# Input projection with its column groups in another order, a gelu in two parts, and low weight parts made by an adding DMA

## The chip, the core and the metric

The kernel runs on one core of one Trainium2 chip. The metric is the device time of one execution in microseconds (us). Three executions of the kernel before took 1475.19, 1468.30 and 1471.88 us; the median is 1471.88 us.

## The reference

The model is a decoder step of two layers for a prompt of 512 tokens and 8 sequences of 4 new tokens. Each layer has a mixing part and a feed-forward part (FFN). In the mixing part one input projection of 1024 to 2048 columns feeds four mixers of width 256, whose outputs are concatenated and go through an output projection:

```python
h = rms_norm(x, p['g_mix_pre'])
z = h @ p['w_in']                                   # 1024 -> 2048
a, ga, u, vb, q, k, v, xd = jnp.split(z, IN_SPLITS, axis=-1)   # eight groups of 256 columns
ya, conv_new = conformer_conv(a, ga, conv_prev, ...)           # depthwise convolution of width 31, LayerNorm
yb, v_rows = chunk_sgu(gelu(u), gelu(vb), ...)                 # u * (tril(W) LN(v) + b)
o = attend(q, k, v, lam)                                       # differential attention
yd, pool_new = pool_mix(xd, ...)                               # window means
mix = jnp.concatenate([ya, yb, yc, yd], axis=-1) @ p['w_out']  # 1024 -> 1024
x = x + rms_norm(mix, p['g_mix_post'])
...                                                            # then the SwiGLU FFN
```

All of it is float32.

## The kernel before

A float32 product is made of three products of a rounded type (fp32r): each operand is split into a high part (the rounded value) and a low part (the rest), and high by high, high by low and low by high are added in PSUM. For a weight tile, `split` (line 189) makes the high part `whi` by a cast on ScalarE (ACT, line 194) and the low part `wlo` by a subtraction, on VectorE (DVE) unless another engine is named (line 197). `whi` and `wlo` are rings of four buffers each in the pool `wp`, and a tile of 128 columns of w_in takes one buffer of each. A group of 256 columns is two tiles. Its raw weights (1 MB, a ring of two buffers) are loaded by the queue of SyncE (SP).

The function `mixing` (line 354) writes the input projection as 15 steps, one for each tile of 128 columns and one for the group at 1536 (the attention's v, which takes two tiles in one step). `order` (line 406) fixes the groups: columns 0 and 256 (convolution), 1280 (k), 1024 (q), 1536 (v), 1792 (pooling), 512 (gating's u), 768 (gating's v). The loop at line 719 does the first 256 tokens of step u, and then the other 256 prompt tokens with the 32 sample tokens (288 columns) of step u-2. So a tile is in use for two steps after its own, and its buffer goes to the tile four places later. The mixers are generators (`conv`, `attention`, `gating`, `pooling`): `advance` moves each active one on between the steps, and those in the list `urgent` are written under a higher priority. A scheduler that simulates the program then fixes the final order of each engine's instructions, from these priorities and from what is ready. PSUM has two banks `acc` for the projections, three `ps`, two `s` and one `oT`, mostly for the attention.

`gating` is started when the last group, 768, is done. It applies gelu to u and v together (lines 592 to 594), then LayerNorm and a product over chunks, then the multiplication by u (line 615), and writes `yb`. The convolution's taps run on DVE (line 427); the rest of `conv` (lines 440 to 464) turns the result, normalises it and writes `ya`. `attention` writes `yc` and `pooling` writes `yd`.

`project_last` (line 1273) then does the output projection: eight turns of 24 matmuls of 512 columns, over the k-tiles in the order `W_OUT_ORDER` = 6, 7 (`yd`), 0, 1 (`ya`), 2, 3 (`yb`), 4, 5 (`yc`). The first turns go to different token tiles, so two of them can be open at once in the `acc` banks.

Of the kernel before, what the change touches and what calls it, by code (L numbers as in the profile page):

```python
# [9 lines left out]
F32R = mybir.dt.float32r  # L10
BF16 = mybir.dt.bfloat16
I32 = mybir.dt.int32
AF = mybir.ActivationFunctionType
ALU = mybir.AluOpType
# [27 lines left out]
AP = 3  # L42

W_OUT_TURNS = [(0, 0), (1, 0), (0, 1), (1, 1), (2, 0), (2, 1), (3, 0), (3, 1)]
W_OUT_ORDER = (6, 7, 0, 1, 2, 3, 4, 5)

PACE_T = 1.0
PACE_A = 0.8
# [74 lines left out]
def trunk(ctx, tc, A, O):  # L123
    nc = tc.nc
    V, S, G, T, SY = nc.vector, nc.scalar, nc.gpsimd, nc.tensor, nc.sync
# [16 lines left out]
    def ps():  # L142
        return psx("ps")
# [210 lines left out]
    def mixing(l, mp, early):  # L354
# [35 lines left out]
        def ev_qk(nm, c, f):  # L390
# [18 lines left out]
            (1280, [(10, ev_qk("k", 0, 10)), (11, ev_qk("k", 1, 11))]),  # L409
            (1024, [(8, ev_qk("q", 0, 8)), (9, ev_qk("q", 1, 9))]),  # L410
            (1536, "v"),
            (1792, [(14, ev_copy(dext[0], 14, 1.0, 15)), (15, ev_copy(dext[1], 15, 1.0, 15))]),
            (512, [(4, ev_copy(uv[:, 0], 4)), (5, ev_copy(uv[:, 1], 5))]),
            (768, [(6, ev_copy(uv[:, 2], 6)), (7, ev_copy(uv[:, 3], 7))]),
        ]


# [12 lines left out]
                    yield  # L430

        convs = []

        def conv():
            for c in range(2):
                while len(convs) <= c:
                    yield
                yield from convs[c]
            o = ps()
            for c in range(2):  # L440
                T.transpose(o[:30, 128 * c:128 * c + 128], hext[c][:, SEQ:SEQ + 30], ident)
            cn = mp.tile([128, SEQ], F32, tag="pt", bufs=3, name="cn")[:, :256]
            S.copy(cn[:30], o[:30, :256])
            SY.dma_start(O[4][l, 0], cn[:30])
            yield
            xn = mp.tile([128, 4, 256], F32, tag="xn", bufs=1, name="xn")
            for t in range(4):
                o = ps()
                for c in range(2):
                    T.transpose(o[:, 128 * c:128 * c + 128], out[c][:, 128 * t:128 * t + 128], ident)  # L450
                mean, r = ln_stats(mp, o[:, :256], 128, "m")
                V.tensor_scalar(xn[:, t, :], o[:, :256], mean, r, op0=ALU.subtract, op1=ALU.mult)
                yield
            y = yp.tile([128, 2, 2, SEQ], F32R, tag="y", name="ya")
            for c in range(2):
                o = ps()
                for t in range(4):
                    T.transpose(o[:, 128 * t:128 * t + 128], xn[:, t, 128 * c:128 * c + 128], ident)
                zh, th = out[c], hext[c][:, 0:SEQ]
                S.activation(zh, o, AF.Identity, scale=pf[:, 72 + c:73 + c], bias=pf[:, 74 + c:75 + c])  # L460
                S.activation(th, zh, AF.Tanh)
                V.scalar_tensor_tensor(zh, th, 1.0, zh, op0=ALU.add, op1=ALU.mult)
                hilo(y, c, zh)
                yield
            Y[0] = y
# [102 lines left out]
        def gating():  # L568
# [20 lines left out]
                mm(o[64 * (h % 2):64 * (h % 2) + 64, 128 * (h // 2):128 * (h // 2) + 128], gr[:, 64 * h:64 * h + 64], wt[:, h, :])  # L589
            V.tensor_tensor(bsg, o[:, :256].rearrange("p (c t) -> p c t", c=2), bsg, op=ALU.add)  # L590
            yield
            for f in (2, 0):
                S.activation(uv[:, f:f + 2], uv[:, f:f + 2], AF.Gelu)
            S.activation(zs[:, 4:8, :], zs[:, 4:8, :], AF.Gelu)
            yield
            vn = mp.tile([128, 4, 256], F32, tag="xn", bufs=1, name="vn")
            for t in range(4):
# [7 lines left out]
            for c in range(2):  # L605
                o = acc()
                for n in range(4):
                    for hh in range(2):
                        h = 2 * c + hh
                        mm(o[64 * hh:64 * hh + 64, 128 * n:128 * n + 128], vn[:, n, 64 * h:64 * h + 64], wt[:, h, :])  # L610
                t = uv[:, 2 + c, :].rearrange("p (n t) -> p n t", n=4)
                V.scalar_tensor_tensor(t, o.rearrange("p (n t) -> p n t", n=4), pf[:, 77 + c:78 + c],
                                       bsg[:, c:c + 1, :].to_broadcast([128, 4, 128]), op0=ALU.mult, op1=ALU.add)
                tf = uv[:, 2 + c, :]
                V.tensor_tensor(tf, tf, uv[:, c, :], op=ALU.mult)
                hilo(y, c, tf)
                yield
# [73 lines left out]
        def load(c0):  # L691
            if c0 == 1536:
                r = rp.tile([128, 8, 256], F32, tag="raw", name="raw")
                SY.dma_start(r, w[:, c0:c0 + 256].rearrange("(k p) f -> p k f", p=128))
                pairs[c0] = [split(r[:, 4 * i:4 * i + 4, :], [128, 4, 256], V) for i in range(2)]
            else:
                pairs[c0] = raw_cols(w, c0, V, early.get(c0), None, G if c0 == 0 and early else None)

        def do_v(t, P, dst):
            o = acc()  # L700
# [18 lines left out]
        for u in range(n + LAG):  # L719
# [19 lines left out]
            if b >= 0:  # L739
# [9 lines left out]
                if c0 == 256 and i == 0:  # L749
                    convs.append(taps(0))  # L750
                    active.append(conv())
                if c0 == 256 and i == 1:
                    convs.append(taps(1))
                if c0 == 1024:
# [5 lines left out]
                        active.append(keys_out())  # L760
                if i == "v":
                    done.add("v")
                if c0 == 768 and i == 1:
                    active.append(gating())
                    urgent.append(active[-1])
# [709 lines left out]
```

## Time and profile before

The profiled execution took 1470.1 us, of which 1468.2 us lie between its first and its last instruction (the span).

| | |
|---|---|
| span | 1468.2 us |
| profiled execution | 1470.1 us |
| median of three | 1471.88 us |
| TensorE (PE) busy | 1393.0 us, 95% |
| DVE busy | 816.3 us, 56% |
| ACT busy | 490.4 us, 33% |
| GpSimd (POOL) busy | 253.9 us, 17% |
| mean granted TensorE clock | 0.981 |

The busy time of PE is that of pipelined matmuls whose ends are modelled, so a stretch in which PE is always busy can still be slow: the granted clock (1.00 is 2.4 GHz, 0.50 is 1.2 GHz) and the spacing of matmuls of one size tell that. What counts for the change is not the share over the whole span but the stretches of the mixing part: the input projection, the stretch between its last matmul and the steady output projection, and the output projection itself. In layer 0 these are about 32 to 156 us, 156 to 181 us and 181 to 232 us; in layer 1 about 758 to 883 us, 883 to 908 us and from there on.

### The profile page before, as it was taken

What the parts mean: (1) busy time and instruction counts of PE and PEld (TensorE: products, weight loads), DVE (VectorE), ACT (ScalarE), POOL (GpSimd) and SP (SyncE); (2) the same over time, 40 slices, a digit from 0 to 9 for tenths busy, and PEclk for the clock granted to TensorE, in tenths of its full rate; (3) what the DMA queues carried; (4) which work ended last, traced back from release to release, by engine and by line L of the source; (5) the groups of instructions that cost most, each with busy time, mean ns of one, the idle gap of its engine ahead of it and who ended that gap; (6) DMA issues with size and microseconds to landing.
All of it is one profiled execution on the core that took longest, in us unless ns stands there. A gap on an engine that the chain in (4) does not pass through costs nothing.

```text
span 1468.2 us, 22964 instructions
## 1 busy us (share of the span) xinstructions
PE 1393.0 (95%) x9274; PEld 1085.7 (74%) x9274; DVE 816.3 (56%) x1624; ACT 490.4 (33%) x972; POOL 253.9 (17%) x271
## 2 busy tenths in 40 slices
PE   6999798989999999999989997989899999999997
PEld 6988677856676777777779886787566677777775
DVE  4997577866424323433669856867564333333344
ACT  4345444322224221222333464433222332222231
POOL 1000245443300000000210004434342000000003
PEclk9999998999999999999999999999999999999999
DMA  6220336786859731323432213378767596213132
GB/s 206 93 87 30 131 117 213 257 299 230 286 177 292 238 137 58 104 69 128 152 115 73 73 53 109 128 244 299 274 235 266 182 299 210 100 58 115 58 133 90
DMA packets 155204, 235.60 MB, mean 160 GB/s; under 512 B 8880, under 2 KB 116410, under 8 KB 155098
## 3 DMA queue, kind: packets, MB, share of 16 engines
q1 hardware_dynamic: 136522, 166.76, 34.8%
q0 software_dynamic: 18432, 67.12, 12.8%
q8 instruction: 73, 1.20, 0.3%
q14 instruction: 33, 0.27, 0.1%
q10 hardware_dynamic: 144, 0.26, 0.0%
HBM read 222.07 MB, written 12.04 MB: 159 GB/s over the span
## 4 chain that ended last, share of the span: by engine, by line
PE 73%; DVE 8%; issue 7%; DMA 6%; POOL 3%; ACT 2%; another core or an unknown queue 0%; SPq 0%; POOLq 0%; DVEq 0%; ACTq 0%
PE acc L128 57%; PE sx L128 8%; DMA kr<-in_cache_k_dram,ik 4%; PE ps L128 2%; PE s L128 2%; DVE sca L886 2%; POOL vr L1030 1%; DVE wlo L197 1%; PE oT L128 1%; POOL kr L1000 1%; DVE m L1315 1%; ACT whi L194 1%; POOL rsw L178 1%; DMA rws<-in_w_gu_dram 1%; PE ps L518 1%
## 5 line engine op out<-in xcount | busy, mean ns | idle before, releaser
L128 PE MATMUL acc<-xhi,whi 128*128 128x512 f32 (+2 forms) x1152 | 409.5, 357 | 3.7 <-issue 1.7
L128 PE MATMUL acc<-xlo,whi 128*128 128x512 f32 (+2 forms) x1152 | 406.7, 353 | 4.2 <-DVE xlo L242 3.2
L128 PE MATMUL acc<-xhi,wlo 128*128 128x512 f32 (+2 forms) x1152 | 407.1, 354 | 0.4 <-issue 0.2
L197 DVE TENSOR_TENSOR wlo<-raw,whi 128x1024 fp32r<-128x1024 f32 x172 | 216.6, 1265 | 198.8 <-ACT whi L194 193.0
L194 ACT CAST whi<-raw 128x1024 fp32r<-128x1024 f32 x178 | 184.3, 1048 | 362.9 <-PE acc L128 320.8
L128 PEld LDWEIGHTS acc<-xhi,whi 128*128 128x128 f32 x1152 | 219.7, 191 | 47.5 <-issue 14.2
L128 PEld LDWEIGHTS acc<-xlo,whi 128*128 128x128 f32 x1152 | 219.9, 191 | 35.8 <-issue 5.7
L128 PEld LDWEIGHTS acc<-xhi,wlo 128*128 128x128 f32 x1152 | 219.6, 191 | 34.6 <-issue 7.9
L128 PE MATMUL acc<-whi,h 128*128 128x512 f32 x704 | 224.7, 396 | 0.6 <-issue 0.6
L128 PEld LDWEIGHTS acc<-whi,h 128*128 128x128 f32 x704 | 131.3, 188 | 44.5 <-issue 11.2
L128 PE MATMUL acc<-wlo,h 128*128 128x512 f32 x352 | 138.4, 395 | 0.0
L1290 POOL TENSOR_TENSOR m<-m,g_g_ffn_post 128x512 f32<-128x512 f32 x14 | 20.2, 1449 | 511.2 <-ACT junk L1289 511.2
L1003 DVE STREAM_TRANSPOSE kt<-kr 128x1024 f32<-128x1024 f32 x64 | 78.3, 1234 | 47.4 <-DMA kr<-in_cache_k_dram,ik 26.9
L1000 POOL DMA_INDIRECT kr<-in_cache_k_dram,ik x64 | 70.3, 1099 | 109.8 <-DVE kt L1003 85.3
L427 DVE SCALAR_TENSOR_TENSOR cacc<-hext,pf,cacc 128x512 f32<-128x512 f32 x120 | 86.9, 745 | 0.8
L128 PEld LDWEIGHTS acc<-wlo,h 128*128 128x128 f32 x352 | 66.1, 188 | 18.0 <-issue 4.6
L1030 POOL DMA_INDIRECT vr<-in_cache_v_dram,iv x64 | 60.5, 945 | 84.7 <-PE sx L128 67.0
L1359 DVE SCALAR_TENSOR_TENSOR th<-th,acc 128x512 f32<-128x512 f32 (+1 forms) x46 | 29.6, 644 | 78.9 <-PE acc L128 78.9
L178 POOL TENSOR_TENSOR rsw<-rsw,mhalf 128x1 f32<-128x1 f32 (+2 forms) x62 | 38.5, 628 | 172.0 <-DVE rsw L177 169.1
L128 PE MATMUL sx<-kt,qs 128*32 128x128 f32 x1024 | 49.3, 278 | 9.3 <-issue 8.6
L554 POOL TENSOR_TENSOR rse<-e,mhalf 128x8 f32<-128x8 f32 x4 | 7.5, 1879 | 257.4 <-DVE e L552 257.4
L1361 ACT CAST h<-th 128x512 fp32r<-128x512 f32 (+1 forms) x48 | 27.9, 582 | 66.5 <-DVE th L1359 58.9
(422 smaller groups left out, 1835.9 us busy)
## 6 DMA issues: line engine op xcount, KB each, us to landing
raw<-in_w_gu_dram SPq DMA_DIRECT2D x44, 1024.0 KB
raw<-in_w_down_dram SPq DMA_DIRECT2D x20, 1024.0 KB
rws<-in_w_gu_dram SPq DMA_DIRECT2D x40, 512.0 KB
raw<-in_w_in_dram SPq DMA_DIRECT2D x16, 1024.0 KB
raw<-in_w_out_dram SPq DMA_DIRECT2D x8, 1024.0 KB
rwo<-in_w_out_dram SPq DMA_DIRECT2D x16, 512.0 KB
rws<-in_w_down_dram SPq DMA_DIRECT2D x16, 512.0 KB
x<-x_t SPq DMA_DIRECT2D x12, 512.0 KB
```

What stands on the lines that cost most here:

```text
L128: T.matmul(out, lhsT, rhs, start=start, stop=stop)
L178: G.tensor_tensor(y, v, mhalf[:P, :n], op=ALU.pow)
L194: S.copy(hi, src)
L197: eng.tensor_tensor(lo, src, hi.bitcast(F32), op=ALU.subtract)
L427: V.scalar_tensor_tensor(a, hext[c][:, t:t + SEQ], pf[:, 8 + 2 * t + c:9 + 2 * t + c], a, op0=ALU.mult, op1=ALU.add)
L886: V.scalar_tensor_tensor(a[:, c], ext[:, c, :, t:t + 4], pf[:, 8 + 2 * t + c:9 + 2 * t + c], a[:, c], op0=ALU.mult, op1=ALU.add)
L1000: G.indirect_dma_start(out=kr, out_offset=None, in_=ck, in_offset=bass.IndirectOffsetOnAxis(ap=ik[:, s, bg:bg + 1], axis=0))
L1003: V.transpose(kt, kr)
L1030: G.indirect_dma_start(out=v.rearrange("p t e -> p (t e)"), out_offset=None, in_=cv, in_offset=bass.IndirectOffsetOnAxis(ap=iv[:, s, a:a + ...
L1290: (V if (t, half) == (3, 1) else G).tensor_tensor(m[t][:, hs], m[t][:, hs], gain[:, hs], op=ALU.mult)
L1359: V.scalar_tensor_tensor(th[:, :n], th[:, :n], 0.5, ou[:, :n], op0=ALU.mult, op1=ALU.mult)
L1361: S.copy(hh, th[:, :n])
```

## The change

The groups after 1536 come in the order 768, 1792, 512 instead of 1792, 512, 768. `gating` so starts when 768 is done, applies gelu to v alone, and waits with gelu of u and the multiplication until 512, now the last group, is done. `conv` enters the list `urgent` once its taps are written. `W_OUT_ORDER` becomes 4, 5, 0, 1, 6, 7, 2, 3. For the six tiles of the groups 768, 1792 and 512, ACT writes the negated cast of the raw weights into `wlo`, a DMA issued by POOL adds the weights from DRAM to it, and ACT writes `whi` as before; the subtraction on DVE is gone.

```diff
-W_OUT_ORDER = (6, 7, 0, 1, 2, 3, 4, 5)
+W_OUT_ORDER = (4, 5, 0, 1, 6, 7, 2, 3)
...
             (1536, "v"),
+            (768, [(6, ev_copy(uv[:, 2], 6)), (7, ev_copy(uv[:, 3], 7))]),
             (1792, [(14, ev_copy(dext[0], 14, 1.0, 15)), (15, ev_copy(dext[1], 15, 1.0, 15))]),
             (512, [(4, ev_copy(uv[:, 0], 4)), (5, ev_copy(uv[:, 1], 5))]),
-            (768, [(6, ev_copy(uv[:, 2], 6)), (7, ev_copy(uv[:, 3], 7))]),
...
+        flow = {}
 
         def conv():
             for c in range(2):
                 while len(convs) <= c:
                     yield
                 yield from convs[c]
+            urgent.append(flow["conv"])
+            yield
             o = ps()
...
-            for f in (2, 0):
-                S.activation(uv[:, f:f + 2], uv[:, f:f + 2], AF.Gelu)
-            S.activation(zs[:, 4:8, :], zs[:, 4:8, :], AF.Gelu)
+            S.activation(uv[:, 2:4], uv[:, 2:4], AF.Gelu)
+            S.activation(zs[:, 6:8, :], zs[:, 6:8, :], AF.Gelu)
...
                                        bsg[:, c:c + 1, :].to_broadcast([128, 4, 128]), op0=ALU.mult, op1=ALU.add)
+                yield
+            while "u" not in done:
+                yield
+            S.activation(uv[:, 0:2], uv[:, 0:2], AF.Gelu)
+            S.activation(zs[:, 4:6, :], zs[:, 4:6, :], AF.Gelu)
+            for c in range(2):
                 tf = uv[:, 2 + c, :]
                 V.tensor_tensor(tf, tf, uv[:, c, :], op=ALU.mult)
                 hilo(y, c, tf)
...
-                pairs[c0] = raw_cols(w, c0, V, early.get(c0), None, G if c0 == 0 and early else None)
+                if c0 not in (768, 1792, 512):
+                    pairs[c0] = raw_cols(w, c0, V, early.get(c0), None, G if c0 == 0 and early else None)
+                    return
+                r = raw_load(w, c0)
+                pairs[c0] = []
+                for i in range(2):
+                    hi = wp.tile([128, 8, 128], F32R, tag="whi", bufs=4, name="whi")
+                    lo = wp.tile([128, 8, 128], F32R, tag="wlo", bufs=4, name="wlo")
+                    src = r[:, :, 128 * i:128 * i + 128]
+                    S.activation(lo, src, AF.Copy, scale=-1.0)
+                    G.dma_start(lo, w[:, c0 + 128 * i:c0 + 128 * i + 128].rearrange("(k p) f -> p k f", p=128), accum_op=ALU.add)
+                    S.copy(hi, src)
+                    pairs[c0].append((hi, lo))
...
+                if c0 == 512 and i == 1:
+                    done.add("u")
```

## Rows read from the trace of the kernel before

**Rows 1.** The page, busy time, share of the span and instructions of the engines.

```profile
PE 1393.0 (95%) x9274; PEld 1085.7 (74%) x9274; DVE 816.3 (56%) x1624; ACT 490.4 (33%) x972; POOL 253.9 (17%) x271
```

**Rows 2.** Stretches: length, busy PE, PEld, DVE, ACT, POOL, clock, DMA share, GB/s.

```profile
74.40:101.70 27.30, 27.22 (x215) 23.72 (x215) 25.78 (x53) 13.81 (x35) 0.00 (x0) 1.00 0.25 77
101.70:156.00 54.30, 54.07 (x417) 46.24 (x415) 37.11 (x92) 31.51 (x80) 2.48 (x2) 1.00 0.18 60
156.04:180.90 24.86, 17.23 (x103) 12.69 (x102) 16.78 (x47) 8.57 (x16) 6.88 (x12) 0.86 0.37 126
180.90:215.50 34.60, 34.60 (x164) 27.99 (x165) 25.82 (x86) 14.12 (x30) 15.47 (x13) 1.00 0.38 123
883.05:908.34 25.29, 17.65 (x105) 12.57 (x103) 16.85 (x47) 8.58 (x16) 7.29 (x12) 0.87 0.40 124
```

**Rows 3.** Waits of PE, 156 to 181 us: total us, times, longest.

```profile
PE acc L128 <- ACT yb L351: 2.7, 1, 2.7
...
PE acc L128 <- ACT ya L351: 1.2, 1, 1.2
```

**Rows 4.** Timeline of PE behind the input projection: start, duration, instruction, count.

```profile
171.10 0.63 PE L128 MATMUL acc<-wlo,ya 128*128 128x512 f32 x1
171.53 0.63 PE L128 MATMUL acc<-whi,ya 128*128 128x512 f32 x1
...
183.53 0.39 PE L128 MATMUL acc<-whi,yc 128*128 128x512 f32 x1
183.76 0.39 PE L128 MATMUL acc<-wlo,yc 128*128 128x512 f32 x1
...
223.16 1.11 PE L239 MATMUL sx<-cst,m 128*128 128x128 f32 x4 [3.43 <-DVE xlo L242]
```

**Rows 5.** Timeline of ACT and DVE: casts, table load and outputs of the mixers.

```profile
74.46 1.04 ACT L194 CAST whi<-raw 128x1024 fp32r<-128x1024 f32 x1 [2.73 <-PE acc L128]
84.80 1.05 ACT L194 CAST whi<-raw 128x1024 fp32r<-128x1024 f32 x1 [1.28 <-PE acc L128]
99.16 1.05 ACT L194 CAST whi<-raw 128x1024 fp32r<-128x1024 f32 x1 [1.01 <-PE acc L128]
...
149.55 1.28 ACT L593 ACT_TABLE_LOAD   x1
150.84 1.06 ACT L593 ACTIVATE uv<-uv 128x1024 f32<-128x1024 f32 x1
...
86.60 1.22 DVE L197 TENSOR_TENSOR wlo<-raw,whi 128x1024 fp32r<-128x1024 f32 x1
...
160.23 0.69 DVE L352 TENSOR_TENSOR yc<-os__1608,yc 128x512 fp32r<-128x512 f32 x1
179.52 1.28 DVE L615 TENSOR_TENSOR uv<-uv 128x512 f32<-128x512 f32 x2
180.88 1.30 DVE L352 TENSOR_TENSOR yb<-uv,yb 128x512 fp32r<-128x512 f32 x2
```

**Rows 6.** Timeline of PE beside the first three casts of rows 5.

```profile
78.48 0.28 PE L128 MATMUL acc<-xhi,whi 128*128 128x256 f32 x1
...
81.44 0.40 PE L128 MATMUL acc<-xhi,whi 128*128 128x288 f32 x1
...
88.50 0.28 PE L128 MATMUL acc<-xhi,whi 128*128 128x256 f32 x1
...
104.53 0.28 PE L128 MATMUL acc<-xhi,whi 128*128 128x256 f32 x1
```

**Rows 7.** Timeline of POOL and DVE: gathers of 512 KB, and who takes them.

```profile
268.36 0.94 POOL L1000 DMA_INDIRECT kr<-in_cache_k_dram,ik  x1 [7.60 <-DVE kt L1003]
271.27 1.66 POOL L1000 DMA_INDIRECT kr<-in_cache_k_dram,ik  x1 [0.73 <-DVE kt L1003]
...
272.98 1.25 DVE L1003 STREAM_TRANSPOSE kt<-kr 128x1024 f32<-128x1024 f32 x1 [0.20 <-PE sx L128]
279.25 1.25 DVE L1003 STREAM_TRANSPOSE kt<-kr 128x1024 f32<-128x1024 f32 x1 [1.05 <-DMA kr<-in_cache_k_dram,ik]
```

More of the change, by code (lines that the diff above doesn't have):

```diff
@@ L751, in mixing @@
                     active.append(conv())
+                    flow["conv"] = active[-1]
                 if c0 == 256 and i == 1:
```

## The prediction

> **What bounds the kernel now.** I read the busy shares first: PE is busy for 95% of the span [rows 1], so a gain has to come from the few stretches where PE waits or runs slowly. The table by stretch shows where these are [rows 2]: in the two stretches of layer 0's input projection PE is busy for 27.22 of 27.30 us and for 54.07 of 54.30 us, at a granted clock of 1.00, and the output projection from 180.9 us on is full as well. Between them lies one stretch, 156.04 to 180.90 us, with 17.23 busy of 24.86 us at a clock of 0.86. Layer 1 has its twin, 17.65 of 25.29 us at 0.87. These two stretches, which I call the tails, are what the change can win from. While the projection itself runs, PE has no free time, so work moved into it makes it longer by its own PE time and gains nothing by itself.
>
> What makes the tail: `gating` starts only behind the last group, and PE waits for each of its steps and for those of `conv`. The waits of PE name `yb` with 2.7 us and `ya` with 1.2 us [rows 3]. The idle time is 24.86 - 17.23 = 7.6 us in layer 0 and 25.29 - 17.65 = 7.6 us in layer 1 [rows 2]. The clock is the other part: at full clock a 512-column matmul follows the last after 0.23 us (183.53 to 183.76), while the twelve with `ya`, behind short work broken by waits, follow at 0.43 us (171.10 to 171.53) [rows 4]. That is the level of 1.2 GHz instead of 2.4. It costs 12 x 0.20 = 2.4 us. A tail loses 7.6 + 2.4 = 10.0 us, both lose 20 us.
>
> **The change, part by part.**
>
> *Order of the groups, early gating, urgent conv, other order of k.* Gating's turns, LayerNorm and product, and conv's end, move into or ahead of the end of the projection. Their PE time stays: of the tail's 17.23 busy us, the 24 matmuls of the output projection are 12 x 0.23 + 12 x 0.43 = 7.9 us, so 9.3 us are mixer work that now ends the projection at about 156 + 9 = 165 us. What has to be there then? `yc` first: its low part is written at 160.23 + 0.69 = 160.9 us [rows 5], 4.9 us behind the old end of the projection. It is early enough for the new one, even with two more table loads at 1.28 us [rows 5] in ACT's queue (gelu between the exponentials and back, in front of the attention). `ya` and `yd` come next, and their steps start sooner than now. The weights of k = 4, 5 take the buffer of 512's first tile, freed one part of 3.4 us (81.44 to 84.80 is one [rows 5, 6]) ahead of the end, and are ready 2.3 us later; those of k = 6, 7 take the second tile's, behind 24 matmuls of cover. `yb` comes last. From the last projection matmul on, its chain is a copy (0.4 us, an estimate from the 1.05 us of a four times larger cast), the table load 1.28, gelu 1.06, the sample gelu 0.3 (an estimate, a small one), two multiplications 1.28, a first cast 0.6 (half of 1.05 and its start) and the low parts 1.30 [rows 5]: 6.2 us. The cover is the two open turns over k = 4, 5, 0, 1, 6, 7: 2 x 18 matmuls x 0.23 = 8.3 us. So `yb` is free; without the cover (one open turn) it would cost 2 us per layer. This part therefore gives the whole 10.0 us per layer, 20 us in all. I take this and not more, although small bubbles inside the busy time could add 1 to 2 us per layer.
>
> The transition into the FFN is not touched: PE waits there too (3.43 us in front of 223.16 [rows 4]), behind DVE work that moves with the output projection. I put it at nothing, with 2 us either way.
>
> *Negated cast and adding DMA.* DVE loses six subtractions of 1.22 us per layer [rows 5], 7.3 us; ACT gets six more casts of 1.05 us, 6.3 us. DVE is busy for 25.78 of 27.30 us and 37.11 of 54.30 us there, ACT for 13.81 and 31.51 us [rows 2], so ACT has 36 us free and the cast is hidden; PE bounds the stretch, so DVE's relief gains nothing directly. POOL was idle in the first stretch and busy 2.48 us in the second, so the issue has room. Behind its wait for ACT are queued the powers of the LayerNorms and of the attention, for which DVE waits; none is late at the new end. The DMA engines carry 3 MB more per layer at a share of 0.25 and 0.18 [rows 2].
>
> What counts is the latency: a tile's buffer is freed by the tile four places before, and until now the tile is ready one cast and one subtraction later, 1.05 + 1.22 = 2.3 us. Now it is the negated cast, the issue, the transfer and its landing. No row shows an adding DMA. The nearest are POOL's gathers of the same 512 KB [rows 7]: the one issued at 268.36 was used at 272.98, at most 4.6 us later; the one issued at 271.27 was waited for until 279.25, 8.0 us later, with the queues loaded. With the cast that is 5.7 to 9.1 us. The addition has to read the tile too, so the upper end is the slower gather twice, 1.05 + 16 = 17 us; the lower end is cast and issue alone, 1.05 + 0.94 = 2.0 us. I take 8 us: the transfer part of the quick gather, 4.6 - 0.94 = 3.7 us, stretched by the second read but not doubled, since these stretches have little other traffic.
>
> How much of that is covered depends on the tile, and the old trace shows what PE had to fill with:
> - 768, first tile: it takes the buffer that is freed at 74.46 [rows 5]. PE did other work until 78.48, 4.0 us [rows 6], and the second part of the tile before (81.44 to 84.80, 3.4 us) can go ahead: 7.4 us. Stall 0.6 us.
> - 768, second tile: buffer at 84.80, next run at 88.50, 3.7 us; two parts of 3.0 us (78.48 to 81.44 is one) of the first tile and of v can go ahead: 9.7 us. No stall.
> - 1792, first tile: buffer from v at 99.16, the tile's run at 104.53 with PE never idle: 5.4 us, the part before included. Stall 2.6 us.
> - 1792, second tile, and both of 512: a whole step lies between, 3.0 + 3.4 + some 3.5 us of attention, 9.9 us. No stall.
>
> That is 3.2 us per layer, 6.4 us in all; at 5.7 us latency 0.3 per layer, at 10 us 2.6 + 0.3 + 4.6 = 7.5, at 12 us 4.6 + 2.3 + 6.6 + 3 x 2.1 = 19.8 us per layer.
>
> The Trainium skill ("DMA: Bandwidth & Descriptors", section "Anatomy of one DMA — SWDGE (gpsimd) path") fits a DMA issued by GpSimd as 2.0 us plus the bytes at 436 GB/s: an estimate of 3.2 us for 512 KB. By it the stall would be nothing and the sum 20 us; the gather that took 8.0 us does not bear that out [rows 7]. Against the change speaks "SBUF — State Buffer", section "Summary: rules for kernel authors": descriptors written by GpSimd are starved while DVE is in its fast modes. The two issues of 0.94 and 1.66 us [rows 7] leave 0.7 us for that; by it the three first tiles would each wait up to 0.7 us more, and the sum would be 4 us worse.
>
> **The sum.** 1470.1 us of the profiled execution - 20.0 + 6.4 = 1456.5 us. The median of the runs shown is 1.8 us above that execution, so I predict 1458 us.
>
> **The rivals.**
> 1. *Nothing stalls*: the latency is 5.7 us or less, or the scheduler finds filler for it. For it speaks the gather of 4.6 us. 1471.9 - 20 = 1452 us, with the small bubbles down to 1448.
> 2. *The gain is eaten*: the latency is about 10 us (7.5 us per layer), or the change does not do what it says, because the fixed order of PE puts steps of conv, attention or gating behind the projection again and PE waits for `yc` or `ya` in place of `yb`. For it speaks that `yc` came 4.9 us behind the last projection matmul. 1471.9 - 20 + 15 = 1467 us, and up to 1472.
> 3. *Slower*: the latency of the adding DMA is 12 us or more. Then PE, which works in a fixed order, stands at the first matmul that needs `wlo` for nearly every tile, with the whole queue behind it. It costs 19.8 us per layer for 10 won: 1471.9 + 19.6 = 1491 us. It decides from the point where the stalls reach 10 us, at a latency of 10.4 us (3.0 + 0.7 + 5.0 + 3 x 0.5). For it speaks that the addition reads both sides and that 8.0 us was seen for a plain gather; against it, that the queues are quiet there.
>
> **How the numbers follow.** Chances: my forecast 0.45, rival 1 0.20, rival 2 0.17, rival 3 0.18. The range takes in rivals 1 and 2 and the nearer part of rival 3: 1446 to 1488 us. By 0.5%, which is 7.4 us and about what a measurement of this kernel can tell from no change, rival 1 (0.20) and the forecast but for its upper edge (0.41) are faster, with 0.02 of rival 2: 0.63. The rest of rival 2 (0.15) and that edge (0.04) are the same: 0.19. Rival 3 is slower: 0.18.
>
> **What would show it.** Right: in the stretch behind the last projection matmul PE's idle time falls from 7.6 to under 2 us per layer, the clock stays near 1.00 there, the waits for `yb`, `vn` and `ya` are gone, and the projection shows a few waits of PE on a DMA into `wlo`, 3 us per layer, mostly at the first tile of 1792. Wrong: waits on that DMA of more than 8 us per layer, at the second tiles too (the latency step), or a wait for `yc` or `ya` at the first matmul of the output projection (the order step), or idle time of PE in the FFN transition that grows by what the tail lost (given back later).

## The result and the profile after

The changed kernel takes 1512.3 us, the median of 4 runs (1502.6 to 1515.4), against 1472.7 us of the kernel before (1468.3 to 1475.2) on the same chip. The ratio is 1.026, with a 95% interval of 1.021 to 1.032. It is slower by some 40 us where 1458 was forecast. Its profiled execution took 1509.9 us with a span of 1508.2.

The stretches of layer 0 show at once that the loss is no single stall. The columns are those of [rows 2]: length, busy PE, PEld, DVE, ACT, POOL, clock, DMA share, GB/s.

```profile
74.10:108.65 34.55, 31.27 (x223) 26.59 (x222) 27.48 (x61) 17.79 (x40) 5.91 (x4) 0.95 0.47 93
108.65:155.60 46.95, 40.68 (x269) 32.11 (x270) 18.01 (x60) 27.39 (x68) 7.07 (x5) 0.83 0.51 95
155.60:191.40 35.80, 29.00 (x215) 26.11 (x214) 22.68 (x55) 7.68 (x16) 7.33 (x11) 0.94 0.10 31
191.40:204.50 13.10, 8.49 (x28) 6.11 (x27) 7.64 (x14) 11.83 (x19) 1.16 (x1) 0.74 0.72 255
204.50:239.00 34.50, 34.33 (x169) 27.76 (x168) 26.36 (x67) 17.33 (x38) 18.01 (x15) 1.00 0.41 137
```

Before, PE was full and at clock 1.00 until 156 us, and there was one tail of 24.86 us [rows 2]. Now PE is idle for 3.3 us in the first of these stretches and for 6.3, 6.8 and 4.6 us in the next three, at clocks of 0.95, 0.83, 0.94 and 0.74. The output projection is full from 204.5 us, where it was from 180.9; both kernels have done 24 of its 192 products by then. The first four stretches are 23.9 us longer than those of [rows 2] from 74.40 to 180.90. Of these, 13.0 are idle time of PE (21.0 us here, 7.9 there), and 10.9 are busy time: 109.4 us here and 98.5 there for the same number of matmuls, 735 in both. The longer busy time goes with the lower clock. Layer 1 has the same pattern.

The waits of PE in the whole span (total us, times, longest) answer to [rows 3]:

```profile
PE acc L128 <- DMA wlo<-in_w_in_dram: 9.3, 5, 3.0
PE acc L128 <- ACT ya L351: 9.2, 2, 4.6
...
PE ps L128 <- DVE rb L559: 5.3, 2, 2.6
PE acc L128 <- DVE vn L604: 5.0, 2, 2.5
...
PE ps L128 <- ACT sq L547: 2.7, 2, 1.3
PE acc L128 <- POOL wt L584: 2.4, 2, 1.4
```

The wait for `yb` is gone, as forecast. The one for `ya` is 4.6 us per layer and was 1.2. `rb` and `sq`, two steps of attention's end, are new. The adding DMA costs PE 9.3 us in both layers.

Where the projection went is seen in PE's timeline of layer 0 (start, duration, instruction, count, and in brackets the idle time before it). The fences after it have a row of ACT, one of SP's DMA queue, and the wait of that queue in both layers (total us, times, longest).

```profile
128.27 0.29 PE L128 MATMUL acc<-xhi,wlo 128*128 128x288 f32 x1
...
149.11 1.15 PE L128 MATMUL ps<-cst,sq 128*128 128x2 f32 x8 [1.33 <-ACT sq L547]
152.89 0.76 PE L128 MATMUL ps<-cst,rb 128*128 128x128 f32 x2 [2.63 <-DVE rb L559]
...
155.58 1.06 PE L581 MATMUL acc<-cst,wn 128*128 128x128 f32 x4
...
158.56 0.66 PE L128 MATMUL acc<-wt,sgr 128*64 128x128 f32 x8 [1.36 <-POOL wt L584]
159.15 0.39 PE L128 MATMUL acc<-xhi,whi 128*128 128x256 f32 x1
...
199.62 0.80 PE L128 MATMUL acc<-whi,ya 128*128 128x512 f32 x1 [4.61 <-ACT ya L351]
```

```profile
148.43 0.63 ACT L547 ACTIVATE sq<-os__1614 128x512 f32<-128x512 f32 x1
...
150.35 0.38 SPq L573 DMA_DIRECT2D wn<-in_sgu_w_dram  x1
```

```profile
SPq L573 <- PE ps L128: 36.2, 2, 19.0
```

From 128.27 to 159.15 us PE issues no matmul of the input projection, though 144 of them are left. It does attention's second half alone. Right behind that half's last step (`rb`) and conv's first transposes stand `gating`'s transposes of `wn` (155.58) and its product with `sgr` (158.56), and only then the projection goes on. `wn` is loaded at 150.35, when PE has read `sq` (149.11 and 1.15 us); SP's queue waited for PE ahead of it, 19.0 us in one of the layers.

The code says why these stand in a row. `gating` is now started behind group 768, with 512 and the second halves of 1792 still to come. Its first step loads `wn` into ring "t512" of three buffers, which attention's `os_`, `sq` and `rb` use too, and takes two banks of ring "acc", which the projection uses. In the order that the scheduler fixed, `wn` gets a buffer only when PE has read `sq`, and `gating`'s two products stand in PE's queue and in ring "acc" ahead of the projection's later parts. So `wn` waits for attention's end, the banks wait for `wn`, and every later part of the projection waits behind them.

### The profile page after: what moved, and what is told of

Read it like the earlier page. It is cut to its first block, busy times and chain, and to the rows that moved or that the text cites. A ratio compares the mean times of both kernels' runs of the same rounds, so it can differ in the third digit from the quotient of the medians.

```text
span 1508.2 us, 23030 instructions
## 1 busy us (share of the span) xinstructions
PE 1411.2 (94%) x9274; PEld 1102.5 (73%) x9274; DVE 806.4 (53%) x1612; ACT 509.6 (34%) x990; POOL 275.4 (18%) x283
## 4 chain that ended last, share of the span: by engine, by line
PE 65%; DVE 12%; issue 11%; DMA 4%; ACT 4%; POOL 2%; another core or an unknown queue 2%; SPq 0%; POOLq 0%; DVEq 0%; ACTq 0%
PE acc L128 50%; PE sx L128 9%; PE ps L128 3%; DVE wlo L197 2%; DVE sca L909 2%; DVE kt L1026 1%; DMA kr<-in_cache_k_dram,ik 1%; DMA wlo<-in_w_in_dram 1%; PE s L128 1%; DVE cacc L427 1%; DVE m L1338 1%; ACT whi L194 1%; DVE x_t L1331 1%; POOL rsw L178 1%
## 5 line engine op out<-in xcount | busy, mean ns | idle before, releaser
L194 ACT CAST whi<-raw 128x1024 fp32r<-128x1024 f32 x166 | 172.2, 1048 | 389.1 <-PE acc L128 333.3
L197 DVE TENSOR_TENSOR wlo<-raw,whi 128x1024 fp32r<-128x1024 f32 x160 | 202.2, 1270 | 186.9 <-ACT whi L194 179.8
L128 PEld LDWEIGHTS acc<-xhi,whi 128*128 128x128 f32 x1152 | 222.8, 194 | 54.9 <-issue 17.1
L128 PEld LDWEIGHTS acc<-xhi,wlo 128*128 128x128 f32 x1152 | 223.3, 194 | 43.7 <-DMA wlo<-in_w_in_dram 10.4
L128 PEld LDWEIGHTS acc<-xlo,whi 128*128 128x128 f32 x1152 | 223.2, 194 | 31.0 <-issue 3.2
L128 PEld LDWEIGHTS acc<-whi,h 128*128 128x128 f32 x704 | 131.3, 188 | 44.2 <-issue 10.9
L715 POOL DMA_DIRECT2D wlo<-in_w_in_dram x12 | 19.1, 1595 | 192.1 <-DVE cacc L427 84.5
L128 PEld LDWEIGHTS sx<-kt,qs 128*32 128x32 f32 x1024 | 30.8, 109 | 27.6 <-issue 21.6
```

The costliest lines, as they stand in the source:

```text
L128: T.matmul(out, lhsT, rhs, start=start, stop=stop)
L194: S.copy(hi, src)
L197: eng.tensor_tensor(lo, src, hi.bitcast(F32), op=ALU.subtract)
L715: G.dma_start(lo, w[:, c0 + 128 * i:c0 + 128 * i + 128].rearrange("(k p) f -> p k f", p=128), accum_op=ALU.add)
```

## The experiments

All of them are compared with the kernel before on the same chip and at the same time, since medians of that one kernel went from 1441 to 1473 us (on one chip it gave 1456 at one time and 1441 at another). Three times read from PE's timelines help, in us: the last projection matmul of layer 0; the first product of the output projection with the last of the four terms `ya` to `yd` in layer 0; and the same in layer 1, counted from that layer's first projection matmul (741.1 us in the kernel before; the projections begin there and at 14.2 us, earlier than the 758 and 32 us given above).

| kernel | last projection matmul | last term, layer 0 | last term, layer 1 | ratio to before (95%) |
|---|---|---|---|---|
| before | 155.8 | 183.5 | 169.8 | 1 |
| the change | 191.3 | 205.9 | 197.1 | 1.026 (1.021 to 1.032) |
| order alone | 191.7 | 206.4 | 192.0 | 1.033 (1.026 to 1.039) |
| DMA alone | 165.8 | 188.2 | 179.3 | 1.012 (1.007 to 1.017) |
| `wn` in ring "pl" | 174.3 | 188.4 | 181.5 | 1.008 (1.005 to 1.011) |
| gating in ring "ps" | 166.0 | 200.6 | 179.6 | 1.014 (1.011 to 1.018) |
| order alone, gating last | 153.9 | 182.1 | 172.2 | 1.004 (1.001 to 1.007) |
| both rings untied, no DMA | 168.2 | 186.9 | 172.9 | 1.005 (1.002 to 1.008) |
| both rings untied, DMA | 174.0 | 189.2 | 177.3 | 1.009 (1.007 to 1.011) |
| 768 second to last | 176.4 | 189.6 | 176.8 | 1.011 (1.007 to 1.014) |
| and conv early | 180.5 | 193.1 | 176.6 | 1.012 (1.009 to 1.014) |
| and pairs, conv as before | 179.0 | 187.8 | 174.5 | 1.005 (1.003 to 1.007) |
| DMA in halves | 166.2 | 191.0 | 177.1 | 1.008 (1.007 to 1.010) |
| pairs on before | 155.7 | 178.2 | 166.9 | 0.993 (0.991 to 0.995) |
| pairs, `yc` second | 155.6 | 179.6 | 165.0 | 0.997 (0.994 to 1.000) |

The change's last terms come 22.4 and 27.3 us later than before, 49.7 us in all where the loss is 40. The other stages were shorter by the rest; this was not taken apart.

### Order or DMA

The first two runs take the change apart. Order alone:

```
-  if c0 not in (768, 1792, 512): ...
-  (... negated cast, adding DMA, cast of the high part ...)
+  pairs[c0] = raw_cols(w, c0, V, early.get(c0), None, G if c0 == 0 and early else None)
```

> The changed order, gelu split and urgent conv stay, but the low parts of 768, 1792 and 512 come from VectorE's subtraction, as in the kernel before: no negated cast, no adding DMA. Theory H (the order holds PE up: gating's first two steps take banks of the projection's ring and wait with them for a buffer that attention's end frees): nearly the whole loss stays. The changed kernel took 1512; its PE waited 9.3 us in all for the adding DMA, so 1512 - 9 = 1503, with 1495 to 1512 as the band; the projection still stands from about 128 to 156 us, and no wait on wlo by DMA is left. Rival D (the adding DMA is what costs, by latency or by what it takes from other transfers): without it the order gives what was forecast for it, 1472.7 - 20 = 1453, band 1446 to 1465.

Measured: 1.033, more than the whole change and above the band of theory H. A stretch of 28 us in this kernel, and the matmuls between which the projection stands:

```profile
128.00:156.00 28.00, 23.23 (x101) 16.22 (x99) 8.74 (x22) 8.87 (x21) 1.64 (x1) 0.50 0.04 11
```

```profile
117.47 0.29 PE L128 MATMUL acc<-xhi,wlo 128*128 128x288 f32 x1
...
154.47 1.06 PE L581 MATMUL acc<-cst,wn 128*128 128x128 f32 x4
...
158.50 0.58 PE L128 MATMUL acc<-xhi,whi 128*128 128x256 f32 x1
```

The stand is there without the DMA, at a clock of 0.50, the level of 1.2 GHz. Rival D is out: the order alone brings the loss. Here the projection stops earlier, at 117.47 us and not at 128.27, but comes back at nearly the same time, 158.50 and 159.15. So in layer 0 the DMA's waits ahead of the stand cost the changed kernel next to nothing: they fall into time that is lost anyway. The intervals of the two ratios overlap, so no gain from the DMA is shown.

DMA alone (the edit above on the kernel before, the other way round):

> The kernel before, with only the low parts of 1792, 512 and 768 made by the negated cast and the adding DMA; the order of the groups, the gelu and the output projection's order are the old ones. Theory H: the old order has 768 last, so gating starts after the last projection part and holds nothing; the DMA costs what PE waits for it, at most the 9.3 us of the changed kernel: 1472.7 + 9 = 1482, band 1472 to 1488. Rival D: the adding DMA brings the whole loss by itself, 1472.7 + 39 = 1512, band 1500 to 1520.

Measured: 1.012, 17 us, a little above the band of H. The waits of PE:

```profile
PE acc L128 <- DMA wlo<-in_w_in_dram: 9.0, 6, 3.3
...
PE acc L128 <- ACT yb L351: 5.4, 2, 2.7
```

The tails' wait for `yb` (2.7 us per layer) is still there, and the DMA's 9.0 us are new. The last terms come 4.7 and 9.5 us later, 14 us of the 17. So the DMA costs more than the 9.0 us that PE is seen to wait for it.

### Which part of the order

Two runs undo one coupling each on the changed kernel, with the DMA kept. `wn` in another ring:

```
-  wn = mp.tile([128, 4, 128], F32, tag="t512", bufs=3, name="wn")
+  wn = mp.tile([128, 528], F32, tag="pl", bufs=3, name="wn")[:, 0:SEQ].rearrange("p (h s) -> p h s", h=4)
```

> The changed kernel with one tile moved: gating's wn takes a buffer of pooling's ring pl, which is free then, and no longer one of ring t512, which attention's end uses. The adding DMA stays. Theory H: gating's first two steps, which take banks of the projection's ring, no longer wait for attention's second half; the projection again lies beside attention, its last part is done at about 160 us and not at 191, and most of the 39.6 us come back: 1512 - 30 to 40, so 1472 to 1482. Gating's normalising steps still take turns with the projection, so the forecast gain of 20 us need not show. Rival D: the time follows the adding DMA and stays at 1505 to 1515. Rival B (the banks alone hold it up, the buffer does not matter): 1500 to 1510.

`gating`'s banks from another ring:

```
-  o = acc()        (four places in gating)
+  o = ps()
```

> The changed kernel with one edit: the four places at which gating takes a bank of the projection's ring take one of attention's ring ps instead. wn stays in ring t512 and still waits for attention's end; the adding DMA stays. Theory H (two conditions together made the projection stand: gating's banks lie in the projection's ring, and its first step waits for attention's buffer): with either one taken away the projection runs on beside attention, so this gives about what moving wn gave, a ratio to before of 1.000 to 1.015, with the projection's last part before 165 us, and gating's steps late, behind attention. Rival B (the buffer alone decides, since gating itself is late either way and the end waits for it): 1.020 to 1.030.

Measured: 1.008 and 1.014. Either edit alone takes away much of the loss: 1.8 of the 2.6% and 1.2 of them. Rivals B and D fall. The first is somewhat above its band (1472 to 1482 us is 1.000 to 1.006), and its last projection matmul is at 174.3 us where 160 was expected; PE waits there for the DMA (9.3 us in both layers) and for `ya` (9.3 us). With the second, the last projection matmul is at 166.0 us, a little past the 165 expected, but `gating` is late, since its own first step still waits for attention.

The third run of this group starts from the order alone and moves one line:

```
-  if c0 == 768 and i == 1:
+  if c0 == 512 and i == 1:
       active.append(gating())
```

> The run with the order alone (no adding DMA), with one line moved: gating is started after the last part of 512, not after the last part of 768. Group 768 still comes two groups earlier than in the kernel before, the gelu is split, the convolution is urgent, the output projection's terms are in the new order; the rings are tied as in the changed kernel. Theory H (the loss lies in where gating's steps stand in program order, ahead of parts of the projection that use the same banks): all but a few us of the loss go, ratio 1.000 to 1.012 where the order alone gave 1.033; the last projection part ends before 165 us. Rival G (another part of the order costs it: the split gelu with its table loads, the urgent convolution, the terms' order): 1.020 to 1.035.

Measured: 1.004 where the order alone gave 1.033. The stretch, and the step that waits for its buffer:

```profile
128.00:156.00 28.00, 27.48 (x193) 22.12 (x191) 19.82 (x42) 16.51 (x38) 0.00 (x0) 1.00 0.12 39
```

```profile
162.49 0.65 PE L581 MATMUL acc<-cst,wn 128*128 128x128 f32 x4 [1.77 <-DMA wn<-in_sgu_w_dram]
```

PE is full again at clock 1.00. `gating`'s first transposes still wait for `wn`, with the rings tied as they were, but no projection stands behind them. So the loss of the order is the place at which `gating` is started; the split gelu, the urgent conv, the earlier 768 and the new order of terms together cost 0.4% when it is started last. Rival G is out.

### Why untying it gives no gain

With the couplings gone the order should have given the 20 us forecast. Here `wn` is in ring "pl", and conv writes its normalised rows into its own accumulators, since `xn` and gating's `vn` share one buffer:

```
-  V.tensor_scalar(xn[:, t, :], o[:, :256], mean, r, op0=ALU.subtract, op1=ALU.mult)
+  for c in range(2):
+      V.tensor_scalar(out[c][:, 128 * t:128 * t + 128], o[:, 128 * c:128 * c + 128], mean, r, ...)
```

> Three edits on the changed kernel: wn in a buffer of ring pl, the convolution branch's normalised rows written in place into its own accumulators (so that it no longer waits for gating's vn to be read), and VectorE's subtraction for all low parts. It computes everything. Theory H: with both rings untied the order gives what was forecast for it without the DMA's waits: 1472.7 - 10 to - 20, so 1453 to 1465, and PE's waits for yb and ya are under 1 us each. Rival C (gating's and the convolution's steps, now beside the projection, cost as much as the two tails gave): 1465 to 1480.

Measured: 1.005, the upper edge of rival C. PE's waits:

```profile
PE acc L128 <- ACT ya L351: 6.8, 2, 3.4
PE acc L128 <- DVE wn L665: 6.8, 2, 3.4
```

No wait for `yb` is left, but pooling's `wn` (a tile of another step with the same name) and conv's `ya` are late, 3.4 us each per layer. Conv's last transposes (176.50 us) stand in PE's order behind pooling's product (174.63), which waited for `wn`. The tail has changed its owner. With the DMA added:

> The changed kernel with both rings untied (wn in pl, the convolution's normalised rows in place) and the adding DMA kept: it differs from the run with both rings untied and VectorE's subtraction by the DMA alone, and from the run with wn in pl by the convolution's rows alone. Theory H with the DMA's price taken from the run that has it alone (1.0118, 17 us for two layers): 1.0048 + 0.006 to 0.012, so 1.011 to 1.017, with 8 to 10 us of PE's waits on wlo. Rival F (beside the new order the DMA's waits fall where PE waits anyway): 1.003 to 1.008, within what the run without the DMA gave.

Measured: 1.009, between the two. The DMA costs 0.4% here, some 6 us, though PE's waits for it are 9.9 us. The two were measured at different times, when the kernel before took 1456 and 1441 us, so the difference is rough.

The next versions start from the one with both rings untied and no DMA. They put pooling first again, as in the kernel before, and 768 second to last:

```
   (1792, ...), (768, ...), (512, ...)
-  W_OUT_ORDER = (4, 5, 0, 1, 6, 7, 2, 3)
+  W_OUT_ORDER = (6, 7, 0, 1, 4, 5, 2, 3)
-  urgent.append(flow["conv"])
```

> A version meant to be faster than both: from the changed kernel, group 768 goes behind 1792 and ahead of 512, wn in a buffer of ring pl, the convolution's normalised rows in place, low parts by VectorE's subtraction, the convolution not urgent, the output projection's terms in the order pooling, convolution, attention, gating. Theory H: pooling is as early as in the kernel before, gating's normalising lies beside the group 512, and of the four terms only the gelu of u and two products come after the projection: of the two tails' 20 us 8 to 16 come back, ratio 0.988 to 0.995. Rival C (the steps now beside the projection cost PE about as much as the tails gave): 0.998 to 1.006.

The same with conv advanced twice as fast:

```
+  pace[active[-1]] = 2        (conv)
```

> As the run with 768 second to last, with one edit more: the convolution branch is advanced two steps for one, so that its normalising stands ahead of attention's second half in program order and takes its banks of ring ps there (its accumulators are done at 112 us in the kernel before, but its normalising begins at 161). Theory H: the convolution's term is ready before the projection ends and no wait for ya is left; 0.985 to 0.993, 2 to 5 us under the run without it. Rival E: the convolution's steps now stand between attention's, attention's end comes later and lies bare behind the projection: 1.000 to 1.010.

Measured: 1.011 and 1.012, worse than all that was expected of the first and a little above rival E's band for the second. Two new costs show in the first. The projection ends late, at 176.4 us, and so `yb` is first used at 189.6, though PE waits for it only 0.7 us in both layers. Four blocks of `gating` stand between parts of the projection there, in a ring of two banks; that their turns are what holds it up was not shown. And the early gelu stands in ACT's queue ahead of attention's `sq`. ACT and PE of the first of the two kernels:

```profile
148.63 0.56 ACT L544 COPY os__1608<-oT 128x512 f32<-128x512 f32 x1
149.21 1.28 ACT L593 ACT_TABLE_LOAD   x1
150.50 1.06 ACT L593 ACTIVATE uv<-uv 128x1024 f32<-128x1024 f32 x1
151.47 0.57 ACT L581 COPY wt<-acc 128x512 f32<-128x512 f32 x1
151.93 0.26 ACT L594 ACTIVATE zs<-zs 128x64 f32<-128x64 f32 x1
152.09 0.62 ACT L545 ACTIVATE sq<-os__1608 128x512 f32<-128x512 f32 x1
```

```profile
152.76 1.86 PE L128 MATMUL ps<-cst,sq 128*128 128x2 f32 x8 [3.86 <-ACT sq L545]
```

PE waits 3.9 us per layer for a square whose input `os_` was ready at 149.2 us; 2.9 of these are the four instructions of `gating` between the two. With conv early, no wait for `ya` is left, but attention's last product with `vtok` moves from 146.9 to 160.9 us, and the projection stands from 130.5 to 157.4. That is rival E's mechanism; its price against the run without the edit lies within the noise.

If the tails are made of chains, shortening the chains should help where reordering does not. Two row blocks go to one bank and share one root on GpSimd, in conv and in `gating` (the edit in short):

```
-  for t in range(4):   o = bank();  2 transposes;  statistics;  root;  subtraction
+  for tp in range(2):  o = bank();  4 transposes;  2 statistics;  one root for both;  2 subtractions
```

On the kernel before:

> The kernel before with another edit: the convolution's and gating's normalising take two row blocks to a bank, one root for both, so two links in place of four in each chain (transpose, statistics, root on GpSimd, subtraction). Same order, no DMA that adds. Theory K (what the two tails lose is the length of these two chains, and no order of the groups shortens them): each of the two chains is some 3 us shorter, 4 to 6 us a layer, ratio 0.992 to 0.996. Rival: the chains are long by their other steps (gelu, casts), 0.998 to 1.002.

Measured: 0.993, as theory K had it; about 10 us less than the kernel before, and the fastest of all. Its PE in the tail of layer 0:

```profile
169.21 3.42 PE L128 MATMUL acc<-wt,vn 128*64 128x128 f32 x32 [2.17 <-DVE vn L617]
172.56 0.78 PE L128 MATMUL acc<-whi,ya 128*128 128x512 f32 x1
...
175.71 0.39 PE L128 MATMUL acc<-whi,yb 128*128 128x512 f32 x1
...
178.20 0.39 PE L128 MATMUL acc<-whi,yc 128*128 128x512 f32 x1
```

The products with `yb` begin at 175.7 us instead of 180.9, and PE does not wait for them; those with `yc` at 178.2 instead of 183.53 [rows 4]. On the version with 768 second to last:

> The version with 768 second to last once more (wn in pl, VectorE's subtraction), with two row blocks to a bank in both normalising steps, so that gating needs two turns with the projection's parts and not four; the convolution's rows are in their own tile again. Theory K: gating's term was late there, at 189.6 us, because its four blocks took turns with four parts of the projection in a ring of two banks; with two turns it is ready by 180, and the last of the four terms is first used 5 to 9 us a layer earlier than there: ratio 0.992 to 1.002. Rival C (the steps beside the projection cost as much as they give wherever they stand): 1.006 to 1.012.

Measured: 1.005, between the two: the pairs give 0.6%, about as much as on the kernel before, but `yb` is at 187.8 us and not at 180. With two turns in place of four the last projection matmul is not earlier, 179.0 us against 176.4, so theory K's reason for the late `yb` is not borne out. PE's waits say what is left:

```profile
PE ps L128 <- ACT sq L558: 7.7, 2, 3.9
PE ps L472 <- DVE xn L466: 7.4, 4, 2.5
```

The square is as late as before, and conv's `xn` shares its buffer with `vn` again, so this run changes two things at once. Then the attempt to fill the tail of the fastest kernel with `yc`, which is ready early:

```
-  W_OUT_ORDER = (6, 7, 0, 1, 2, 3, 4, 5)
+  W_OUT_ORDER = (6, 7, 4, 5, 0, 1, 2, 3)
```

> The run with two row blocks to a bank on the kernel before, with the output projection's terms in the order pooling, attention, convolution, gating. There attention's term is ready at about 161 us and first used at 178, while PE waits for the convolution's until 172.6. Theory K: twelve products of 0.23 us (two turns of 6) come into that gap, 2.8 us a layer, 5.6 in both: 0.9928 - 0.004 = 0.987 to 0.991 against before. Rival: the convolution's transposes come later behind them, and nothing is gained: 0.992 to 0.994.

Measured: 0.997, above both bands: no further gain. The waits for `yb` are back:

```profile
PE acc L128 <- ACT yb L362: 5.4, 2, 2.7
```

`yb` is now the last term. Its first use, 179.6 us, is 1.4 us behind that of the last term without the filler (`yc`, 178.2), and in layer 1 the last term is 1.9 us earlier (165.0 against 166.9): in sum the filler hardly moved the end. The two ratios come from different chips and their intervals touch, so it is not shown either that the filler costs something.

### The DMA's time

> The kernel before with the adding DMA of the run that has it alone, each transfer of 512 KB cut into two of 256 KB (the first four blocks of rows, then the last four). Theory P (the transfer takes its time in proportion to its rows, so the first half lands in about half): PE can start on the first half earlier, its waits on wlo fall from 9.0 to under 5 us, ratio 1.004 to 1.010. Rival Q (the time is a fixed one for each transfer, and GpSimd issues them one behind the other, 1.6 us each): the waits stay or rise to 9 to 14 us, ratio 1.012 to 1.020.

Measured: 1.008, in theory P's range, but PE's waits are 8.6 us in seven pieces, not under 5. The DMA issues of the version with both rings untied, and of this one (size, median us from issue to landing):

```profile
wlo<-in_w_in_dram POOLq DMA_DIRECT2D x12, 512.0 KB, 7.5
```

```profile
wlo<-in_w_in_dram POOLq DMA_DIRECT2D x24, 256.0 KB, 7.3
```

In the median half the bytes take about the same time to land. But the medians hide a spread: in layer 0 the halves took 4.7 to 11.1 us, the whole ones 6.3 to 8.6. The first tile, of group 1792, shows it. This run issues its first half at 76.47 us, and the run with the DMA alone its whole transfer at 76.51. PE's first use of the low part, and of its second half, in this run, and the first use in the run with the DMA alone:

```profile
81.81 0.39 PE L128 MATMUL acc<-xhi,wlo 128*128 128x256 f32 x1
...
84.24 0.38 PE L128 MATMUL acc<-xhi,wlo 128*128 128x256 f32 x1 [0.47 <-DMA wlo<-in_w_in_dram]
```

```profile
84.89 0.58 PE L128 MATMUL acc<-xhi,wlo 128*128 128x256 f32 x1 [2.50 <-DMA wlo<-in_w_in_dram]
```

The first half could be used at most 5.3 us after its issue, the whole transfer after 8.4 us. So a first half can land sooner, and the halves behind it land later. As the two halves are issued one behind the other and share the queue, this does not separate a fixed time from a queue; that stays open. It brought no gain that shows: the last terms come as late as with whole transfers (in sum 368.1 us against 367.5), and the intervals of the two ratios overlap.

For reference, the kernel before on the chip of the runs with gating in ring "ps", with 768 second to last and with conv early:

> The kernel before, unchanged, for a profile on the chip on which the others of this call run. Both theories: a span of 1450 to 1470, two tails before the steady output projection with 7 to 8 us of idle PE between them, and the steady output projection of layer 0 from about 181 us.

Its span was 1439.8 us, below the band expected, with the two tails where they were: the last terms at 183.0 and 170.1 us.

## Why the prediction was wrong

**What bounds the kernel.** Right: the two tails are where time is to be had, and the chains `conv` and `gating` make them. The run with paired blocks was about 10 us faster, and its last terms came 5.3 and 2.9 us earlier.

**The order step failed.** The prediction let `gating`'s steps move into the projection at nothing but their PE time, 9.3 us. It costed what is moved and not what then stands behind it. The moved steps take banks of the projection's ring, and the first of them waits for a buffer that attention's end gives back, so 144 matmuls of cover went behind the very step that they were to cover. The projection was to end at about 165 us and ended at 191.3. Instead of 20 us gained, the order alone lost 3.3%, some 47 us. Rival 2 had the fixed order of PE in it, but with steps of the mixers behind the projection; here the projection was behind the mixers. The mechanism is shown by three runs: another buffer, other banks, and the start moved. Why the order gives nothing even with the rings untied is argued from the waits; no run had both `wn` in another ring and `gating`'s banks outside ring "acc".

**The cover of `ya`.** Of `ya` and `yd` the prediction said that "their steps start sooner than now". But `ya` was first used at 199.6 us, behind a wait of 4.6 us; a wait for `ya` was its sign of a failed order step. The projection's late end is one part of this. ACT's queue in the changed kernel shows another:

```profile
192.83 1.45 ACT L463 ACTIVATE cacc<-ps,pf 128x512 f32<-128x512 f32 x2
194.30 1.28 ACT L619 ACT_TABLE_LOAD   x1
195.59 1.06 ACT L619 ACTIVATE uv<-uv 128x1024 f32<-128x1024 f32 x1
196.55 0.24 ACT L620 ACTIVATE zs<-zs 128x64 f32<-128x64 f32 x1
196.70 1.13 ACT L464 ACTIVATE hext<-cacc 128x512 f32<-128x512 f32 x2
```

**The table loads.** The prediction reckoned with them in front of the attention and in the chain of `yb`, where its sums covered them, but not in front of `ya`. Here the gelu of u, now split off, stands with its table load between the two activations of conv's end, and the second begins 2.4 us after the first has ended (194.28 to 196.70). That is 2.4 of the 4.6 us for which PE waits, by the trace; no run took it apart. With 768 second to last the load and the gelu stood ahead of `sq` instead, 2.9 of 3.9 us per layer.

**The latency term was too small.** The first tile of 768 in the changed kernel:

```profile
74.14 1.05 ACT L716 CAST whi<-raw 128x1024 fp32r<-128x1024 f32 x1 [2.73 <-PE acc L128]
75.09 1.06 ACT L714 ACTIVATE wlo<-raw 128x1024 fp32r<-128x1024 f32 x1
```

```profile
76.47 1.83 POOL L715 DMA_DIRECT2D wlo<-in_w_in_dram  x1 [52.40 <-DVE cacc L427]
```

```profile
84.92 0.47 PE L128 MATMUL acc<-xhi,wlo 128*128 128x256 f32 x1 [2.57 <-DMA wlo<-in_w_in_dram]
```

From the free buffer (74.1) to the first use that waited for it are 10.8 us; the term was 8. The cast of the high part went ahead of the negated one (1.0 us), GpSimd was busy 1.83 us with the issue where 0.94 had been taken, and 8.4 us passed from the issue on. The stall at this tile was 2.6 us, not 0.6. (In the prediction's own list, a latency of 10 us gives 7.8 us per layer and not 7.5, since the three last tiles lack 0.1 us each; nothing hangs on it.) In the sum PE waited 4.7 us per layer, not 3.2; alone on the old order the DMA cost 8.5 us per layer. So the gain forecast would have shrunk to little even if the order had worked. Rival 3 came nearest (1491 us, 1512 measured), but by the wrong mechanism: not a stall at nearly every tile, but one stand.

The Trainium skill ("DMA: Bandwidth & Descriptors", section "Anatomy of one DMA — SWDGE (gpsimd) path") gives 2.0 us plus the bytes at 436 GB/s, by which 512 KB would take an estimated 3.2 us. The trace disagrees: in the version with both rings untied the median from issue to landing is 7.5 us, and in the run with halves it is 7.3 us for half the size. The measurement decides.

The rule of "SBUF — State Buffer", section "Summary: rules for kernel authors", also the Trainium skill, that DVE's fast modes starve descriptors written by GpSimd, had been given 0.7 us a tile. The twelve issues took 1.60 us in the mean, next to 0.94 and 1.66 us of the gathers [rows 7]; whether DVE has a part in that, no run here shows.

**The upper end.** The range ended at 1488 us, in the nearer part of rival 3. No term of the sum stood for a wait of the moved steps themselves, so nothing in it could reach 1512.

## What to carry to other kernels

When a step is moved ahead of other work, list every ring from which it takes a buffer or a bank and ask who used that ring last: its first wait becomes the wait of everything behind it in the engine's order that uses the same rings. Do the same for each engine's queue: a table load with its activation can come to stand between two links of another chain. Here shortening the chain (two blocks to a bank, one root) gave 0.7%, and none of the orders tried gave anything. A transfer that replaces an engine's instruction trades throughput for latency, so cost it from the moment the buffer is free to its first use.

## What was not expected of the hardware

A transfer cut in half did not land sooner in the median: 7.3 us for 256 KB against 7.5 for 512 KB, both added by the DMA into a tile, though single halves landed in 4.7 us. Each issue held GpSimd for about 1.6 us, the two halves of one tile together for 2.6 to 2.9. The granted clock fell to 0.50 over 28 us in which PE was busy for 23.2 us with short matmuls of attention, and stood at 1.00 in the same stretch when projection matmuls lay between them (27.5 us busy). And the same kernel had spans of 1468.2 and 1439.8 us on two chips, while its two mixing stages agreed within 0.5 us (last terms at 183.5 and 183.0 us, 169.8 and 170.1); nearly all of the difference arose at 300 to 390 us and 960 to 1125 us, between the mixing stages and behind them.
